# Where the row scales of two head groups are computed: at the recurrence's end, and at attention's own first pass

## The chip, the cores and the metric

One core of one Trainium2 chip runs the whole kernel. The metric is the device time of one execution in microseconds (us); less is better. A profiled execution gives the span from the first to the last instruction and every instruction's start and end. PE is TensorE, ACT is ScalarE, DVE is VectorE, POOL is GpSimd, SP is the queue that issues the DMAs. A number with L is a line of the kernel.

## The reference

One layer of a decoder trunk over 2048 rows of width 1024, in float32. One input projection feeds two head groups: a gated linear recurrence (4 heads of 128) and a stick-breaking attention (8 heads of 64). What the change touches is the normalisation of each group's output by rows, and the output projection behind it:

```python
o_hg = rmsnorm(o_hg, hg_out_norm) * silu(hg)        # 512 columns, eps 1e-6
o_sb = rmsnorm(o_sb, sb_out_norm)                   # 512 columns
mix  = concatenate([o_hg, o_sb], axis=-1) @ w_out   # 1024 x 1024
h    = h + rmsnorm(mix, attn_post_norm)
```

with rmsnorm(x, w) = x * rsqrt(mean(x*x) + eps) * w. The scale rsqrt(mean + eps) is one number a row and group. A dense SwiGLU layer and a gated per-layer embedding follow.

## The kernel before, in words

The 2048 rows are worked in four groups g of 512 rows, and each group in four blocks t of 128 rows. Gains are folded into the operands, and the row scale of a group's half is applied to the product instead of to the operand: half the contraction of the output projection (the recurrence's 512 columns, part 0) is multiplied by the scale of the recurrence's rows, the other half (attention's columns, part 1) by that of attention's rows.

The recurrence (hgrn, L493 to L607) runs head by head. Each head adds the square of its output to a tile acc (L594, L597). After the last head, PE multiplies acc by a column of ones (L605), which gives the sum of squares of each row in the bank hg, and ACT copies these four columns to hgss[:, g, :] (L606), which lives through the whole kernel.

Attention's outputs are loaded by out_load (L612), which writes the operands and adds the squares of attention's half to the tile oss (L626, L629). It is called one group ahead: for g + 1 before the pass of g begins.

The output projection out_proj (L634), called a pass here, starts with sums (L638): four products of oss with the ones in the bank tr (L641), two DVE copies that put the recurrence's sums and attention's sums side by side into the tile rg of eight columns (L643, L644), then on POOL a multiplication and addition (sum / 512 + eps, L645) and a power of -0.5 (L646). Then come four quarters of 256 columns, in each of them part 0 and part 1. A part multiplies four 128x128 blocks by both halves of the rows into two banks of 512 columns. ACT evicts part 0 with the recurrence's scale (L672), DVE adds part 1 with attention's scale (L674). Every product is three matmuls (L224, L225, L226) of operands split into a high part (cast on ACT, L210) and a low part (a subtraction on DVE or POOL, L211).

The order of PE's instructions is written out by hand. The work is cut into steps by generators, and weave (L50) interleaves them: while a pass runs, each of its steps is preceded by a step of attention and one of the recurrence for the next groups, in the passes g = 0 and 1, and by pieces of the normalisation of the mixed rows (post_mix) and of transposes (turn) in later ones. A pass has 32 steps; the first four are part 0 of the first quarter, and the fifth begins part 1. An attention step is either one that makes scores and weights (weights_of, L404: bank z, then ACT L416 and L417, a scan on DVE L431, a product on POOL L435), or one that multiplies the values and turns the next weights (values_of, L459 and L460; turn_of: transposes into the bank tr at L443, read by ACT L446 and DVE L448). A recurrence step makes scores at L525 from a tile qp that POOL updates (L562).

The bank tr has one buffer, for attention's transposes, for the sums and, in the last pass, for every second transpose of turn (L747, read by ACT L752). The bank mm has three.

The other engines' order is not written out: a planner takes instructions, as they become ready in its own model of time, by the order of the program. A tile's new owner waits until the old one's readers are done.

Of the kernel before, what the change touches and what calls it, by code (L numbers as in the profile page):

```python
# [8 lines left out]
F32 = mybir.dt.float32  # L9
# [3 lines left out]
AF = mybir.ActivationFunctionType  # L13
ALU = mybir.AluOpType

P = 128
# [5 lines left out]
TT = GT // P  # L22
HH = 4
# [4 lines left out]
EPS = 1e-6  # L28
# [61 lines left out]
def hybrid_block(  # L90
# [6 lines left out]
    nc = tc.nc  # L97
# [28 lines left out]
    const = ctx.enter_context(tc.tile_pool(name="const", bufs=1))  # L126
# [3 lines left out]
    def ctile(name, shape, dt=F32, pool=const):  # L130
        return pool.tile(list(shape), dt, tag=name, name=name)
# [13 lines left out]
    neghalf = ctile("neghalf", (P, 1))  # L145
# [21 lines left out]
    hgss = ctile("hgss", (P, NG, TT))  # L167
# [6 lines left out]
    def bank(tag):  # L174
        return ps.tile([P, 512], F32, tag=tag, name=tag, bufs=BANKS[tag])
# [12 lines left out]
    def ev(dt=F32, name="ev", shape=(P, GT)):  # L188
        return fb.tile(list(shape), dt, tag="ev", name=name, bufs=12)
# [61 lines left out]
    def dense_op(w_cols, act):  # L251

        ws = [weight(w_cols(kk)) for kk in range(0, HH, 2)]
        banks = []
        for i in range(2):
            banks.append(mm_bank())
            for kk in range(HH):
                mv = [t[:, kk % 2 * 256:(kk % 2 + 1) * 256] for t in ws[kk // 2]]
                for j in range(2):
                    mm3(banks[i][:, j * 256:(j + 1) * 256], cut(act[kk], 2 * i + j), mv,  # L260
                        kk == 0 and j == 0, kk == HH - 1 and j == 1)
                if kk == 1:
                    yield None
            yield banks[i]

    def row_rstd(halves, out=None, ss=None):
        if ss is None:
            ss = const.tile([P, 2], F32, tag="ss", name="ss", bufs=8)
            for j, y in enumerate(halves):
                nc.scalar.activation(junk, y, AF.Square, scale=ROOT, accum_out=ss[:, j:j + 1])  # L270
        r = const.tile([P, 1], F32, tag="ssum", name="ssum", bufs=8)
        nc.gpsimd.tensor_scalar(r, ss[:, 0:1], ss[:, 1:2], EPS, op0=ALU.add, op1=ALU.add)
        if out is None:
            out = const.tile([P, 1], F32, tag="rstd2", name="rstd2", bufs=6)
        nc.gpsimd.tensor_tensor(out, r, neghalf, op=ALU.pow)
        return out
# [216 lines left out]
    def hgrn(g):  # L493
        acc = None
        for h in range(HH):
            def ht(tag, bufs=1, shape=(P, TT, P)):
                return hgp.tile(list(shape), F32, tag=tag, name=tag, bufs=bufs)
# [44 lines left out]
            for w in LEVELS:  # L542
                if w < BL:
                    level(qp, masks[w])
                else:
                    if w == BL:
                        b = bank("hg")
# [30 lines left out]
            for c in range(TT - 1):  # L578
                nc.vector.scalar_tensor_tensor(
                    st[:, c, :], states[-1], last[:, c:c + 1], sbk[:, c * P:(c + 1) * P],  # L580
                    op0=ALU.mult, op1=ALU.add)
# [10 lines left out]
            if h == 0:  # L592
                acc = ht("acc")
# [9 lines left out]
        b = bank("hg")  # L603
        for c in range(TT):
            nc.tensor.matmul(b[:, c:c + 1], acc[:, c, :], ones1, start=True, stop=True)  # L605
        nc.scalar.copy(hgss[:, g, :], b[:, 0:TT])  # L606
        yield  # L607

    HG_STEPS = HH * 11 + 2
# [23 lines left out]

    def out_proj(g, res):  # L634
        ops, acc = res["o"], res["oss"]
        r_hg, r_sb = [], []

        def sums(acc):  # L638
            b = bank("tr")
            for t in range(TT):  # L640
                nc.tensor.matmul(b[:, t:t + 1], acc[:, t * P:(t + 1) * P], ones1, start=True, stop=True)  # L641
            rr = const.tile([P, 2 * TT], F32, tag="rg", name="rg", bufs=2)
            nc.vector.tensor_copy(rr[:, 0:TT], hgss[:, g, :])  # L643
            nc.vector.tensor_copy(rr[:, TT:], b[:, 0:TT])  # L644
            nc.gpsimd.tensor_scalar(rr, rr, 1.0 / (HH * P), EPS, op0=ALU.mult, op1=ALU.add)  # L645
            nc.gpsimd.tensor_tensor(rr, rr, neghalf.to_broadcast((P, 2 * TT)), op=ALU.pow)  # L646
            r_hg.extend(rr[:, t:t + 1] for t in range(TT))
            r_sb.extend(rr[:, TT + t:TT + t + 1] for t in range(TT))

        sums(acc)  # L650
        mix = [[None, None] for _ in range(TT)]
        for quarter in range(4):
            half, o = divmod(quarter, 2)
            if o == 0:
                for t in range(TT):
                    mix[t][half] = ev(name="mix")
            for part in range(2):
                def src(k, part=part, c=quarter * 256):
                    r = (part * HH + k) * P
                    return w_out[r:r + 2 * P, c:c + 256]  # L660

                bank_no = 0
                for b in dense_op(src, ops[part * HH:(part + 1) * HH]):
                    if b is None:
                        yield
                        continue
                    for n in range(2):
                        t = 2 * bank_no + n
                        d = mix[t][half][:, o * 256:(o + 1) * 256]
                        bn = b[:, n * 256:(n + 1) * 256]  # L670
                        if part == 0:
                            nc.scalar.activation(d, bn, AF.Copy, scale=r_hg[t])  # L672
                        else:
                            nc.vector.scalar_tensor_tensor(d, bn, r_sb[t], d, op0=ALU.mult, op1=ALU.add)  # L674
                    bank_no += 1
                    yield
                if g == NG - 1 and o == 1 and part == 1:
                    for t in range(TT):
                        m = mix[t][half]
                        nc.sync.dma_start(h2_s[g][t * P:(t + 1) * P, half * GT:(half + 1) * GT], m)  # L680
                        nc.scalar.activation(junk, m, AF.Square, scale=ROOT, accum_out=sums_m[:, 2 * t + half:2 * t + half + 1])
        res["mix"] = mix
        if g == NG - 1:
            for t in range(TT):
                row_rstd(None, rows_m[t], sums_m[:, 2 * t:2 * t + 2])
# [488 lines left out]
    class Rate:  # L1174
# [29 lines left out]
        ("a", 3, 40, 21), ("b", 2, 52, 26), ("b", 3, 54, 42),  # L1204
    ]
    hgs = [Stream(hgrn(g)) for g in range(NG)]
    spent = 0
    for n, (kind, g, att_n, hg_n) in enumerate(plan):
# [33 lines left out]
    for g in range(NG - 1):  # L1242
        if g + 1 < NG - 1:
            out_load(g + 1, res[g + 1])
        op = Stream(out_proj(g, res[g]))
        if g == 0:
            weave(op, 2, rates.part(2), r2.part(2))
            hgs[2].drain()
            weave(op, OP_SLOTS - 2, rates.part(OP_SLOTS - 2), r3.part(OP_SLOTS - 2))
        elif g == 1:  # L1250
            weave(op, half, rates.part(half), r3.part(half), (pm, TT, 0))
            tu = Stream(turn(un_s[0], u_s[0], g_ffn, ["mm"], xt, ev))
            weave(op, half, rates.part(half), r3.part(half), (tu, 9, 0))
            hgs[3].drain()
            att_stream.drain()
            side.close()
            big[0] = ctx.enter_context(tc.tile_pool(name="bigr", bufs=1, side="right"))
            mm_tags[:] = ["mm", "z", "mm", "z", "mm", "av"]
        else:
            out_load(NG - 1, res[NG - 1])  # L1260
            weave(op, half, (pm, TT, 0))
            weave(op, half, (Stream(first_operands()), ND, 1))
        op.drain()
        pm = Stream(post_mix(g, res[g]["mix"]))

    drive = Drive([(gate_up(0, tt0), 3), (down(0), 4), (gate_up(1, tt1), 3), (down(1), 4),
                   (ple(0, ss0), 5), (ple(1, ss1), 5)])
    drive.prepare(2)
    op = Stream(out_proj(NG - 1, res[NG - 1]))
    tu = Stream(turn(un_s[1], u_s[1], g_ffn, ["tr", "hg"], xt, ev))  # L1270
    weave(op, half + 2, (pm, TT, 0), (tu, 9, 0))
# [40 lines left out]
    for g in range(NG):  # L1312
        stage, step, every, lag, tag = (
            (1, 67, 2, 3, "mm"), (2, 0, 1, 2, "hg"), (3, 67, 2, 3, "mm"), (4, 0, 1, 4, "hg"))[g]
# [35 lines left out]
```

## Time and profile before

| | us |
|---|---|
| median of 3 runs | 3018.2 (3015.58 to 3018.63) |
| the profiled execution's own time | 3020.01 |
| its span, first to last instruction | 3018.0 |
| PE busy | 2913.6 |
| DVE busy | 2086.6 |
| ACT busy | 1579.3 |
| POOL busy | 1431.3 |

The granted clock of TensorE was 0.99 of the full one over the span. In lines of a timeline the first two numbers are the start and the length in us, then engine, line, operation, out<-in by the program's names, the shape, the number of instructions merged; square brackets hold the idle time of that engine just before, and what ended it. In a view of a tile or line, three numbers are the least, median and greatest duration in ns, followed by the first and last start in us. A line of the waits names who waited for whom, the us in total, the times, and the longest. A row of a table by stretches holds the stretch, its length, the busy us of PE, PE's weight loads, DVE, ACT and POOL with their instructions, the granted clock, the DMA share and GB/s.

### The profile page before, as it was taken

How to read it: one execution, taken by the hardware profiler on the slowest of the kernel's cores; microseconds unless marked ns; L12 is line 12 of the kernel's file. 1: busy time of each engine (PE TensorE's matmuls, PEld its weight loads, DVE VectorE, ACT ScalarE, POOL GpSimd, SP SyncE). 2: the span in 40 equal slices, each digit the busy share in tenths (PEclk: the TensorE clock that was granted, in tenths of full speed). 3: DMA queues.
4: the chain of work that ended last, by engine and by line, in shares of the span. 5: the costliest groups of instructions: out<-in, count | busy, mean ns of one | idle time of the engine just before them, and what ended most of it. 6: DMA issues, size and time to landing. Idle time of an engine off the chain costs nothing.

```text
span 3018.0 us, 52849 instructions
## 1 busy us (share of the span) xinstructions
PE 2913.6 (97%) x18280; PEld 2423.3 (80%) x18280; DVE 2086.6 (69%) x2945; ACT 1579.3 (52%) x3188; POOL 1431.3 (47%) x1398
## 2 busy tenths in 40 slices
PE   7999999999999999889998999999999999999998
PEld 6888788878787888789786878888888888878777
DVE  3556666677777776765887787665887775756775
ACT  5666756666667666767523333455433333545532
POOL 3344455545556666865422322445732221456553
PEclk9999999999999999999999999999999999999999
DMA  7775665455445444468767767667955555677974
GB/s 209 223 217 154 177 181 163 148 173 163 142 137 160 146 132 142 160 199 281 260 218 255 248 216 253 208 203 213 344 191 167 173 176 172 213 218 237 321 242 148
DMA packets 469420, 602.28 MB, mean 200 GB/s; under 512 B 43168, under 2 KB 277664, under 8 KB 469152
## 3 DMA queue, kind: packets, MB, share of 16 engines
q1 hardware_dynamic: 469152, 598.91, 63.1%
q8 instruction: 144, 2.36, 0.3%
q14 instruction: 124, 1.02, 0.1%
HBM read 439.89 MB, written 158.86 MB: 198 GB/s over the span
## 4 chain that ended last, share of the span: by engine, by line
PE 45%; DMA 5%; DVE 4%; POOL 2%; issue 2%; ACT 1%; SPq 0%; POOLq 0%; DVEq 0%; ACTq 0%
PE mm L224 6%; PE mm L226 6%; PE mm L225 6%; PE z L226 4%; PE z L225 4%; PE z L224 4%; PE av L226 2%; PE av L225 2%; PE av L224 2%; PE tr L224 2%; PE tr L226 2%; PE tr L225 2%; DVE wl L813 1%; DMA wr<-in_w_out_dram 1%; DVE wr L817 1%
## 5 line engine op out<-in xcount | busy, mean ns | idle before, releaser
L812 ACT CAST wh<-wr 128x512 fp32r<-128x512 f32 x600 | 351.0, 618 | 466.2 <-PE mm L225 185.6
L813 POOL TENSOR_TENSOR wl<-wr,wh 128x512 fp32r<-128x512 f32 x256 | 373.1, 1464 | 444.0 <-ACT wh L812 418.8
L435 POOL TENSOR_TENSOR a<-be,ring 128x512 f32<-128x512 f32 (+2 forms) x320 | 319.1, 998 | 416.0 <-DVE ring L431 394.8
L224 PE MATMUL mm<-uh,wh 128*128 128x512 f32 x1168 | 484.3, 415 | 2.8 <-DVE eb L336 1.8
L226 PE MATMUL mm<-uh,wl 128*128 128x512 f32 x1168 | 460.6, 394 | 0.4 <-POOL wl L211 0.4
L225 PE MATMUL mm<-ul,wh 128*128 128x512 f32 x1168 | 459.0, 393 | 0.0
L813 DVE TENSOR_TENSOR wl<-wr,wh 128x512 fp32r<-128x512 f32 x344 | 302.1, 886 | 172.6 <-ACT wh L812 158.0
L431 DVE TENSOR_TENSOR_SCAN ring<-z,ring,be 128x512 f32<-128x512 f32 x192 | 245.6, 1279 | 107.0 <-ACT z L417 104.1
L224 PE MATMUL mm<-wh,uh 128*128 128x256 f32 (+1 forms) x992 | 307.2, 310 | 9.6 <-ACT uh L812 9.6
L226 PE MATMUL mm<-wh,ul 128*128 128x256 f32 (+1 forms) x992 | 292.1, 294 | 0.0
L225 PE MATMUL mm<-wl,uh 128*128 128x256 f32 (+1 forms) x992 | 292.0, 294 | 0.0
L226 PEld LDWEIGHTS mm<-uh,wl 128*128 128x128 f32 x1168 | 220.4, 189 | 51.6 <-POOL wl L211 0.8
L224 PEld LDWEIGHTS mm<-uh,wh 128*128 128x128 f32 x1168 | 221.8, 190 | 45.4 <-DVE eb L336 2.3
L225 PEld LDWEIGHTS mm<-ul,wh 128*128 128x128 f32 x1168 | 221.8, 190 | 39.8
L210 ACT CAST wh<-wr 128x512 fp32r<-128x512 f32 x288 | 178.3, 619 | 140.0 <-PE mm L225 79.5
L448 DVE TENSOR_TENSOR al<-tr,ah 128x512 fp32r<-128x512 f32 (+1 forms) x320 | 192.3, 601 | 80.7 <-ACT ah L446 79.8
L211 POOL TENSOR_TENSOR wl<-wr,wh 128x512 fp32r<-128x512 f32 x144 | 190.3, 1322 | 108.6 <-ACT wh L210 98.0
L813 POOL TENSOR_TENSOR wl<-s,wh 128x512 fp32r<-128x512 f32 x44 | 95.3, 2171 | 272.2 <-ACT wh L812 249.3
L446 ACT CAST ah<-tr 128x512 fp32r<-128x512 f32 (+1 forms) x320 | 167.7, 524 | 104.3 <-PE tr L443 101.1
L416 ACT ACTIVATE be<-z 128x512 f32<-128x512 f32 (+2 forms) x320 | 171.1, 535 | 84.1 <-PE z L414 35.6
L224 PEld LDWEIGHTS mm<-wh,uh 128*128 128x128 f32 x992 | 190.0, 192 | 18.0 <-ACT uh L812 10.4
L225 PEld LDWEIGHTS mm<-wl,uh 128*128 128x128 f32 x992 | 190.3, 192 | 5.0
(313 smaller groups left out, 7246.5 us busy)
## 6 DMA issues: line engine op xcount, KB each, us to landing
wr<-in_w_gate_up_dram SPq DMA_DIRECT2D x308, 256.0 KB, 3.8
wr<-in_w_in_dram SPq DMA_DIRECT2D x224, 256.0 KB, 3.1
wr<-hid_s SPq DMA_DIRECT2D x154, 256.0 KB, 3.0
wr<-in_w_down_dram SPq DMA_DIRECT2D x110, 256.0 KB, 3.5
hid_s<-hs SPq DMA_DIRECT2D x88, 256.0 KB, 3.5
wr<-wd_s SPq DMA_DIRECT2D x88, 256.0 KB, 3.1
kt<-k_s SPq DMA_DIRECT2D x80, 256.0 KB, 3.1
vt<-v_s SPq DMA_DIRECT2D x80, 256.0 KB, 3.4
```

The costliest lines, as they stand in the source:

```text
L210: nc.scalar.copy(hi, src)
L211: (lo_engine or nc.gpsimd).tensor_tensor(lo, src, hi.bitcast(F32), op=ALU.subtract)
L224: nc.tensor.matmul(o, l[0], r[0], start=start, stop=False)
L225: nc.tensor.matmul(o, l[0], r[1], start=False, stop=False)
L226: nc.tensor.matmul(o, l[1], r[0], start=False, stop=stop)
L416: nc.scalar.activation(be[:, :n], z[:, :n], AF.Sigmoid, scale=0.125)
L431: nc.vector.tensor_tensor_scan(r[:, o:o + n][:, ::-1], z[:, :n][:, ::-1], be[:, :n][:, ::-1], init, op0=ALU.mult, op1=ALU.bypass)
L435: nc.gpsimd.tensor_tensor(a[:, :n], be[:, :n], r[:, o + 1:o + n + 1], op=ALU.mult)
L446: nc.scalar.copy(hi[:, lo_c:], tr[:, lo_c:])
L448: nc.vector.tensor_tensor(lo[:, lo_c:], tr[:, lo_c:], hi[:, lo_c:].bitcast(F32), op=ALU.subtract)
L812: nc.scalar.copy(hi, src)
L813: lo_engine.tensor_tensor(lo, src, hi.bitcast(F32), op=ALU.subtract)
```

## The change

The recurrence's end no longer copies the sums: ACT scales them by 1/512 while it takes them out of the bank, and POOL adds eps and takes the power, in place, so that hgss holds scales. The pass uses them directly. Its sums are made for attention's half alone, when part 1 of the first quarter begins (the fifth step), and the multiplication and addition are done by DVE while it reads the bank; POOL keeps the power, now of four columns.

```diff
@@ hgrn
         for c in range(TT):
             nc.tensor.matmul(b[:, c:c + 1], acc[:, c, :], ones1, start=True, stop=True)
-        nc.scalar.copy(hgss[:, g, :], b[:, 0:TT])
+        r = hgss[:, g, :]
+        nc.scalar.activation(r, b[:, 0:TT], AF.Copy, scale=1.0 / (HH * P))
+        nc.gpsimd.tensor_scalar(r, r, EPS, None, op0=ALU.add)
+        nc.gpsimd.tensor_tensor(r, r, neghalf.to_broadcast((P, TT)), op=ALU.pow)
         yield
@@ out_proj
         ops, acc = res["o"], res["oss"]
-        r_hg, r_sb = [], []
+        r_hg, r_sb = [hgss[:, g, t:t + 1] for t in range(TT)], []
 
         def sums(acc):
             b = bank("tr")
             for t in range(TT):
                 nc.tensor.matmul(b[:, t:t + 1], acc[:, t * P:(t + 1) * P], ones1, start=True, stop=True)
-            rr = const.tile([P, 2 * TT], F32, tag="rg", name="rg", bufs=2)
-            nc.vector.tensor_copy(rr[:, 0:TT], hgss[:, g, :])
-            nc.vector.tensor_copy(rr[:, TT:], b[:, 0:TT])
-            nc.gpsimd.tensor_scalar(rr, rr, 1.0 / (HH * P), EPS, op0=ALU.mult, op1=ALU.add)
-            nc.gpsimd.tensor_tensor(rr, rr, neghalf.to_broadcast((P, 2 * TT)), op=ALU.pow)
-            r_hg.extend(rr[:, t:t + 1] for t in range(TT))
-            r_sb.extend(rr[:, TT + t:TT + t + 1] for t in range(TT))
-
-        sums(acc)
+            rr = const.tile([P, TT], F32, tag="rg", name="rg", bufs=2)
+            nc.vector.tensor_scalar(rr, b[:, 0:TT], 1.0 / (HH * P), EPS, op0=ALU.mult, op1=ALU.add)
+            nc.gpsimd.tensor_tensor(rr, rr, neghalf.to_broadcast((P, TT)), op=ALU.pow)
+            r_sb.extend(rr[:, t:t + 1] for t in range(TT))
+
         mix = [[None, None] for _ in range(TT)]
         for quarter in range(4):
...
             for part in range(2):
+                if quarter == 0 and part == 1:
+                    sums(acc)
+
                 def src(k, part=part, c=quarter * 256):
```

## The prediction

> **What bounds the kernel.** I read the page's totals first.
>
> ```profile
> span 3018.0 us, 52849 instructions
> PE 2913.6 (97%) x18280; PEld 2423.3 (80%) x18280; DVE 2086.6 (69%) x2945; ACT 1579.3 (52%) x3188; POOL 1431.3 (47%) x1398
> ```
>
> TensorE (PE) is the bound: 3018.0 - 2913.6 = 104.4 us without a matmul is all that a better order can win. The change touches the four output projections, g = 0 to 3. Each begins with its sums (L641), the first near 1147 us and the last near 1401; the view of that line and the first pass's piece of the timeline:
>
> ```profile
> L641 PE MATMUL tr<-ones,oss x32: 168/250/352, 1147.0 to 1401.9; 128*128 128x1 f32 x32
> ...
> 1146.95 0.95 PE L641 MATMUL tr<-ones,oss 128*128 128x1 f32 x8
> ```
>
> The table by stretches for 1140 to 1460 us (its sum), and the list of PE's waits there, longest first:
>
> ```profile
> sum 320.00, PE 290.31 PEld 268.92 DVE 212.94 ACT 219.15 POOL 204.09; mean PE 72.58 PEld 67.23 DVE 53.23 ACT 54.79 POOL 51.02
> ...
> PE av L460 <- DVE al L448: 6.1, 2, 4.8
> ...
> PE hg L525 <- POOL qp L562: 2.9, 3, 2.2
> ...
> PE hg L589 <- DVE sl L585: 2.5, 3, 1.1
> ...
> PE tr L747 <- DVE rg L644: 0.8, 1, 0.8
> PE hg L525 <- DVE ks L564: 0.8, 1, 0.8
> ```
>
> PE idles 320 - 290.31 = 29.7 us in these stages, and no row says that PE waits for the sums' input. So the sums' own matmuls (0.95 us a pass, at either place) are neither saved nor added. What can change is who waits for their result, and what they wait for at the new place.
>
> **What the scales cost now.** The view of the tile rg, and the power of a single column from the view of its line:
>
> ```profile
> L643 DVE COPY rg<-hgss x4: 136/166/1027, 597.6 to 1345.2; 128x4 f32<-128x4 f32 x4
> L645 POOL TENSOR_SCALAR rg<-rg x4: 203/390/592, 1150.3 to 1405.9; 128x8 f32<-128x8 f32 x4
> L646 POOL TENSOR_TENSOR rg<-rg,neghalf x4: 1656/1666/1840, 1151.4 to 1406.2; 128x8 f32<-128x8 f32 x4
> ...
> L275 POOL TENSOR_TENSOR rstd<-ssum,neghalf x56: 539/562/1107, 8.9 to 2808.3; 128x1 f32<-128x1 f32 x56
> ```
>
> A power takes 0.562 us for one column and 1.666 for eight, so (1.666 - 0.562)/7 = 0.158 us for each more, and about 0.562 + 3 x 0.158 = 1.04 for four: an estimate from these two medians. POOL now spends 0.39 + 1.67 = 2.06 us a group in one piece at the head of the pass. Afterwards it spends an addition (taken as the same 0.39) and 1.04 at the recurrence's end, and 1.04 later for attention's half: 2.47, or 4 x 0.41 = 1.6 us more in all. It gains only by where it lies. DVE loses four copies, 0.14 to 1.03 us each.
>
> **Pass g = 1, the gain.** POOL, then ACT and PE, and last how PE's bank tr comes free:
>
> ```profile
> 1251.27 0.58 POOL L645 TENSOR_SCALAR rg<-rg 128x8 f32<-128x8 f32 x1
> ...
> 1254.74 1.84 POOL L646 TENSOR_TENSOR rg<-rg,neghalf 128x8 f32<-128x8 f32 x1
> ...
> 1258.85 0.83 POOL L562 TENSOR_TENSOR qp<-qp,pd 128x256 f32<-128x256 f32 x1
> ...
> 1256.61 0.84 ACT L672 ACTIVATE mix<-mm,rg 128x256 f32<-128x256 f32 x2 [2.00 <-POOL rg L646]
> ...
> 1257.02 0.49 PE L443 MATMUL tr<-ident,a 128*128 128x128 f32 x3
> 1259.73 0.46 PE L525 MATMUL hg<-qp,ks 128*32 128x32 f32 x32 [2.22 <-POOL qp L562]
> ...
> 1260.68 0.51 ACT L446 CAST ah<-tr 128x384 fp32r<-128x384 f32 x1
> ...
> 1261.74 0.55 DVE L448 TENSOR_TENSOR al<-tr,ah 128x384 fp32r<-128x384 f32 x1
> ```
>
> ACT's queue stands for 2.00 us at the first eviction (L672) because POOL finishes the power at 1256.58; POOL itself is 0.58 + 1.84 = 2.42 us later at qp, and PE waits 2.22 for qp. With the recurrence's scales ready long before, both waits go: -2.2 us.
>
> But the sums come back at this very place. The second part starts right behind this L525 (fifth step of the pass), and its sums need the only bank tr. The transposes that filled it end at 1257.51, and al has read it at 1261.74 + 0.55 = 1262.29: 4.78 us, of which ACT's 2.00 goes, leaving 2.8. Less the L525 between (0.46), PE waits 2.3. Term: -2.2 + 2.3, taken as 0. Bounds: with the quickest turnaround shown in the next fence it is -2.2 + 0.9 = -1.3; with no relief of ACT -2.2 + 4.3 = +2.1.
>
> **Pass g = 0, the new wait.** Quickest case first, then the place where the fifth step begins:
>
> ```profile
> 1149.74 0.60 PE L443 MATMUL tr<-ident,a 128*128 128x128 f32 x4
> 1151.00 0.69 DVE L448 TENSOR_TENSOR al<-tr,ah 128x512 fp32r<-128x512 f32 x1 [1.02 <-ACT ah L446]
> ...
> 1159.81 0.60 PE L443 MATMUL tr<-ident,a 128*128 128x128 f32 x4
> 1160.34 0.46 PE L525 MATMUL hg<-q,ks 128*32 128x32 f32 x32
> ...
> 1162.05 0.59 ACT L446 CAST ah<-tr 128x512 fp32r<-128x512 f32 x1
> ...
> 1163.23 0.67 DVE L448 TENSOR_TENSOR al<-tr,ah 128x512 fp32r<-128x512 f32 x1
> ```
>
> In the quick case tr is free 1151.69 - 1150.34 = 1.35 us after the transposes; at the new place at 1163.90, or 3.1 us after L525 ends at 1160.80. PE's queue behind the sums holds the second part's matmuls, then the next score matmuls (L410) and recurrence steps: all stand. Nothing is won in this pass, since ACT doesn't wait for rg here. Term: +3.1 (from +0.9, which is 1.35 - 0.46, to +3.1).
>
> **Pass g = 2.** Here POOL lies on the chain:
>
> ```profile
> 1346.26 0.59 POOL L645 TENSOR_SCALAR rg<-rg 128x8 f32<-128x8 f32 x1
> ...
> 1347.83 1.67 POOL L646 TENSOR_TENSOR rg<-rg,neghalf 128x8 f32<-128x8 f32 x1
> ...
> 1350.10 0.30 POOL L272 TENSOR_SCALAR ssum<-ss 128x1 f32<-128x1 f32 x1
> ...
> 1353.59 1.64 POOL L699 TENSOR_TENSOR h<-h,mix 128x512 f32<-128x512 f32 x1 [1.29 <-DVE mix L698]
> 1355.19 1.71 POOL L211 TENSOR_TENSOR wl<-wr,wh 128x512 fp32r<-128x512 f32 x1
> ...
> 1348.58 0.19 ACT L270 ACTIVATION_READ_ACCUMULATOR junk<-mix 128x1 f32 x1
> ...
> 1356.96 0.58 PE L225 MATMUL z<-wl,uh 128*128 128x256 f32 x1 [4.42 <-POOL wl L211]
> ```
>
> PE waits 4.42 us for a weight's low part, which stands on POOL behind additions that wait for the row scale of L272; L645 and L646 (2.26 us) are ahead of it. The square that L272 sums is ready at 1348.77, so L272 can move from 1350.10 by 1.3 us at most: -1.3 (bounds 0 and -2.3). No attention is left in this pass, so tr is free for the sums. The new power (1.04) becomes ready just about when that weight stands on POOL: ahead of it, it takes 1.04, behind it nothing; +0.5. Sum -0.8.
>
> **Pass g = 3.**
>
> ```profile
> 1405.88 0.33 PE L747 MATMUL tr<-ident,xt 128*128 128x128 f32 x1 [0.78 <-DVE rg L644]
> ...
> 1408.91 0.69 ACT L752 ACTIVATE ev<-tr,g_ffn 128x512 f32<-128x512 f32 x1
> ...
> 1409.24 0.60 PE L747 MATMUL hg<-ident,xt 128*128 128x128 f32 x4
> ```
>
> The transposes no longer wait for the sums' copy: -0.8. In turn the sums, behind the second L747, wait until L752 has read tr at 1409.60; since PE arrives there earlier by 0.78 and by the moved sums, between 0 and 1.7 us: +1.0. Sum +0.2.
>
> **The recurrence's ends.** The addition and power (1.43 us, four times) go on POOL where it has pauses; the evictions that read them come later. Cover: POOL's 320 - 204 = 116 idle us here. +0.2 (0 to 1.4, should one stand ahead of a qp).
>
> **The clock.** Granted clock in the stretch behind PE's wait of 2.22 us, and behind that of 4.42:
>
> ```profile
> 1260.00:1263.00 3.00, 3.00 (x39) 2.58 (x25) 2.28 (x5) 3.00 (x9) 2.83 (x3) 0.64 0.27 80
> ...
> 1357.00:1360.00 3.00, 3.00 (x15) 3.00 (x16) 2.43 (x3) 2.47 (x6) 1.59 (x1) 0.53 1.05 397
> ```
>
> So a wait of 2.22 loses another 3.0 x 0.36 = 1.1 us, one of 4.42 loses 1.4. For the new 3.1 at g = 0 I add 1.3 (0 to 1.4); at g = 1 one such wait replaces another. The Trainium skill (TensorE: Matmul & The Clock Gate, Part 1: The HAM clock gate) says that the clock halves after an idle window of about 3.4 us and returns after as long a busy one. By that rule this term is nothing and the sum 1.3 lower; the row behind 2.22 us speaks against the rule's length, so I keep the term.
>
> **What is given back.** While PE stands at g = 0, ACT, DVE and POOL catch up, and the waits listed for sl (2.5) and ks (0.8) shrink: -1.5 of the 3.3 (0 to -3.3).
>
> **Sum:** g = 0: 3.1 + 1.3; g = 1: 0; g = 2: -0.8; g = 3: +0.2; ends +0.2; given back -1.5: +2.5 us. The profiled execution took 3020.01 us (span 3018.0), so 3022.5; the median of the runs is 3018.2, 1.8 less, and on that scale I forecast 3020.7. Against the noise of this kernel (0.2%, or 6 us, is about what a measurement can tell from no change) that is no change. Ends of the terms: low 0.9 - 1.3 - 2.3 - 0.8 - 3.3 = -6.8, high 3.1 + 1.4 + 2.1 + 1.0 + 0.9 + 1.4 = +9.9.
>
> **Rivals.**
> Freed POOL carries (faster). If the planner lets tr be read early, each new wait is 0.9 and costs no clock: g = 0 +0.9; g = 1 -1.3 and its dip's -1.1; g = 2 the full -2.3 and a shorter wait's -1.4; g = 3 -0.8: -6.0, or 3012. For it: POOL is named in the waits of both passes. Against: ACT runs in order and needed 1.6 us to reach ah at g = 0. Chance 0.17.
> The bank tr decides (slower). PE stands behind the sums at full length: +3.1 + 1.4, at g = 1 +2.1 + 0.6, at g = 2 nothing, at g = 3 +0.9, ends +1.4, nothing given back: +9.5, or 3027.7. It decides from a turnaround of about 2.7 us on, since from a wait of 2.2 the clock falls too; both places had more (3.5 and 4.78). Against: the helpers catch up. Chance 0.21.
> The planner re-orders (either sign). Only PE's order is written out; L643 for g = 0 ran at 597.6, far ahead of its pass at 1147. New entries on POOL and ACT shift everything behind, and if a third of the 29.7 idle us moves, that is 10 us either way: 3008 or 3028. Chance 0.08.
>
> **Numbers.** The forecast keeps 0.54. Faster by over 0.2% takes half of the first rival, half of the last and a little of the forecast's edge: 0.14. Slower takes most of the second, half of the last, an edge of the forecast: 0.23. Same: 0.63. The range, 3010 to 3029, holds the sum's two ends (3011.4 and 3028.1) and most of the planner's.
>
> **What would show it.** Right: L641 idle before it on PE at g = 0 and 1, released by DVE al; no ACT wait for a scale at L672; PE's 2.22 for qp gone; 1.0 us for the four-column power. Wrong: no wait at L641, PE's 4.42 at g = 2 gone, or idle time moved in stages that the change doesn't touch, before 1140 or after 1480 us.

## The result, and the profile after

The changed kernel takes 3035.45 us (median of 4 runs, 3033.19 to 3036.23), the kernel before in the same session 3018.41 (4 runs, 3015.58 to 3020.79): a ratio of 1.0051, 95% interval [1.0039, 1.0063]. It is slower by 17 us; I forecast 3020.7 and at most 3029. The profiled execution took 3036.23. The totals of its page:

```profile
span 3034.2 us, 52841 instructions
PE 2920.6 (96%) x18280; PEld 2430.1 (80%) x18280; DVE 2085.6 (69%) x2941; ACT 1578.0 (52%) x3188; POOL 1435.1 (47%) x1402
```

PE is busy 7.0 us longer with the same 18280 matmuls, and the granted clock over the span was 0.987 instead of 0.990; the other 9.2 us of the 16.2 are idle time. The small operations came out as costed, as the views of the tiles rg and hgss show:

```profile
L646 DVE TENSOR_SCALAR rg<-tr x4: 148/162/163, 1170.3 to 1430.4; 128x4 f32<-128x4 f32 x4
L647 POOL TENSOR_TENSOR rg<-rg,neghalf x4: 1011/1016/1041, 1170.6 to 1430.6; 128x4 f32<-128x4 f32 x4
...
L608 POOL TENSOR_SCALAR hgss<-hgss x4: 233/240/244, 597.7 to 1354.9; 128x4 f32<-128x4 f32 x4
L609 POOL TENSOR_TENSOR hgss<-hgss,neghalf x4: 1015/1042/1052, 598.0 to 1355.7; 128x4 f32<-128x4 f32 x4
```

A power of four columns takes 1.02 to 1.04 us. The cost is elsewhere. PE's order is written out, so the n-th matmul of one kernel (sums and fillers left out) is the n-th of the other. I took its start in each profile and subtracted: the difference at a place is the time lost up to there. Worked out so, with places in us of the kernel before, for this kernel and those of the experiments below:

```
                900   1140   1300   1400   1700   3010     span
changed         1.1    2.5   15.4   19.7   16.7   15.7   3034.2
e_again         1.7    2.4   12.0   15.0   12.5   13.4   3031.8
e_head         -0.4    1.6    6.5    6.1    8.6    8.3   3026.8
e_late_only     0.4    2.4    8.3   12.1    9.5    9.9   3028.3
e_step6         1.5    3.8    5.6    8.6    5.2    3.6   3021.9
e_mm_clean      0.8    3.5    5.4    9.6    9.7    9.9   3028.9
e_mm_bank      -0.4    0.9    2.1    5.8    8.0   18.7   3037.4
e_move_only    -0.4    2.2   10.7   15.4   17.0   10.9   3029.7
e_move_mm       1.1    2.0    5.1    9.6   11.7    4.8   3022.8
e_fill          1.2    4.1   10.8   14.8   13.7   21.1   3039.6
e_fill_again    1.2    3.5    9.4   13.4   10.2   17.1   3035.5
e_swap          0.3   -0.1    3.8    4.0   -0.6   -0.4   3017.6
e_actcopy       2.2    1.9    3.1    3.5    3.5    3.1   3021.1
e_ends_only     3.1    4.4    4.4    3.4    4.3    0.3   3019.5
e_read_ends     2.4    2.8    2.7    2.7    2.3   -4.0   3014.0
```

These are single executions; up to 900 us, where hardly anything differs, they lie between -0.4 and 3.1, so a difference under some 3 us says little. The rows changed and e_again are two executions of one kernel, and they differ by 3.3 us between 1140 and 1300 alone. The changed kernel's loss lies where the change is, between 1140 and 1400 us: 17.2 us in the passes g = 0, 1 and 2, and 12.6 in e_again. The table by stretches splits it, first before, then changed over the same matmuls (columns as above):

```profile
1140.00:1240.00 100.00, 92.25 (x1047) 82.05 (x1047) 70.06 (x112) 67.72 (x145) 67.62 (x80) 0.98 0.41 129
1240.00:1300.00 60.00, 52.52 (x575) 46.89 (x576) 45.52 (x69) 45.05 (x104) 49.75 (x61) 0.91 0.56 186
1300.00:1400.00 100.00, 91.35 (x867) 87.18 (x866) 62.47 (x91) 67.17 (x144) 60.74 (x58) 0.97 0.73 239
```

```profile
1142.50:1251.20 108.70, 96.80 (x1047) 85.92 (x1047) 70.94 (x112) 67.70 (x145) 66.80 (x81) 0.93 0.39 119
1251.20:1315.40 64.20, 53.69 (x576) 48.38 (x577) 46.52 (x66) 45.84 (x104) 50.77 (x61) 0.88 0.56 188
1315.40:1419.70 104.30, 93.22 (x866) 88.93 (x865) 61.67 (x91) 66.77 (x143) 59.00 (x57) 0.95 0.67 221
```

The first column after the length is PE's busy time. Pass 0 is 8.7 us longer: 4.15 more idle (11.90 against 7.75) and 4.55 more busy, with the clock at 0.93 instead of 0.98. Pass 1 is 4.2 longer, 3.0 idle and 1.2 busy; pass 2 4.3 longer, 2.4 idle and 1.9 busy. The first two have their main cause in the timeline, at the sums of pass 0 and then of pass 1:

```profile
1165.13 0.46 PE L525 MATMUL hg<-q,ks 128*32 128x32 f32 x32
...
1167.65 0.67 DVE L448 TENSOR_TENSOR al<-tr,ah 128x512 fp32r<-128x512 f32 x1
...
1168.47 1.84 PE L644 MATMUL tr<-ones,oss 128*128 128x1 f32 x8 [2.88 <-DVE al L448]
...
1268.33 0.46 PE L525 MATMUL hg<-qp,ks 128*32 128x32 f32 x32
...
1271.70 0.54 DVE L448 TENSOR_TENSOR al<-tr,ah 128x384 fp32r<-128x384 f32 x1
...
1272.38 1.84 PE L644 MATMUL tr<-ones,oss 128*128 128x1 f32 x8 [3.60 <-DVE al L448]
...
1294.31 1.08 PE L536 MATMUL hg<-qp,ks 128*64 128x64 f32 x8 [2.45 <-DVE ks L564]
```

PE waits 2.88 and 3.60 us for al to read the bank tr, as the rival of the bank had it. The wait for qp in front of L525 is gone (it was 2.22), and a new one of 2.45 for ks has come later in the pass. The longest rows of PE's waits in these two passes, and two shorter ones:

```profile
PE av L460 <- DVE al L448: 6.9, 3, 4.7
PE tr L644 <- DVE al L448: 6.5, 2, 3.6
PE av L459 <- ACT ah L446: 3.3, 2, 2.5
PE hg L536 <- DVE ks L564: 2.4, 1, 2.4
...
PE hg L605 <- POOL acc L597: 0.9, 1, 0.9
...
PE hg L525 <- DVE ks L564: 0.7, 1, 0.7
```

Before, the rows of L460 and L459 were 6.1 and 3.2, and the 0.9 for acc, at the recurrence's end in pass 0, was not there. And the clock ahead of the first of the two waits and behind it, in stretches cut where it changes:

```profile
1160.88:1164.29 3.41, 3.41 (x15) 3.22 (x15) 0.78 (x2) 1.02 (x4) 3.24 (x7) 0.50 0.79 224
...
1167.70:1174.53 6.83, 6.06 (x55) 5.38 (x55) 0.78 (x3) 0.49 (x1) 1.62 (x2) 0.50 0.10 25
```

PE works again from 1168.47, and to 1174.53 the clock is 0.50: about 6.1 us at half speed, so here the wait of 2.88 us costs about another 3.0; the sums themselves take 1.84 us instead of 0.95. In e_again a wait of 3.15 us at the same place cost some 1.7. The low stretch behind it, and then the one behind the 2.22 us of the kernel before:

```profile
1168.00:1171.40 3.40, 3.40 (x17) 3.40 (x17) 0.16 (x1) 0.00 (x0) 1.01 (x1) 0.50 0.12 34
```

```profile
1260.82:1264.23 3.41, 2.93 (x40) 2.21 (x41) 1.47 (x3) 3.06 (x9) 3.23 (x5) 0.50 0.48 140
```

In all sixteen traces a stretch at 0.50 lasts 3.41 us or two to four times that, but for the last one of each trace, which its end cuts short. So the clock behind a wait comes in steps of some 1.7 us of lost work, and a wait of about 3 us cost one step in one execution and nearly two in the other. The stretch from 1160.88 lies ahead of the sums; e_again has none there, so it is no part of the bank's price.

### The profile page after: what moved, and what is told of

Its sections match the earlier page's. It is cut to its first block, busy times and chain, and to the rows that moved or that the text cites. A ratio compares the mean times of both kernels' runs of the same rounds, so it can differ in the third digit from the quotient of the medians.

```text
span 3034.2 us, 52841 instructions
## 1 busy us (share of the span) xinstructions
PE 2920.6 (96%) x18280; PEld 2430.1 (80%) x18280; DVE 2085.6 (69%) x2941; ACT 1578.0 (52%) x3188; POOL 1435.1 (47%) x1402
## 4 chain that ended last, share of the span: by engine, by line
PE 38%; DMA 4%; DVE 3%; issue 2%; POOL 2%; ACT 1%; SPq 0%; POOLq 0%; DVEq 0%; ACTq 0%
PE mm L224 5%; PE mm L226 5%; PE mm L225 5%; PE z L226 3%; PE z L224 3%; PE z L225 3%; PE av L224 2%; PE av L226 2%; PE av L225 2%; PE tr L224 2%; PE tr L226 2%; PE tr L225 2%; DMA wr<-in_w_gate_up_dram 1%; POOL wl L815 1%; DVE wl L815 1%
## 5 line engine op out<-in xcount | busy, mean ns | idle before, releaser
L815 POOL TENSOR_TENSOR wl<-s,wh 128x512 fp32r<-128x512 f32 x44 | 103.1, 2348 | 261.6 <-ACT wh L814 209.2
```

The source lines that it names most:

```text
L815: lo_engine.tensor_tensor(lo, src, hi.bitcast(F32), op=ALU.subtract)
```

## The experiments

Theories: the bank tr with the clock behind its wait (passes 0 and 1); the new work on POOL at the recurrence's ends; the later power in pass 2; and the planner, which orders ACT, DVE and POOL anew whenever an instruction moves. Four sessions; each session's kernels are compared with runs of the kernel before on the same chip.

**First session: one part at a time.** e_head leaves the scales at the recurrence's end and puts attention's sums back at the head of the pass:

```diff
+        sums(acc)
         mix = [[None, None] for _ in range(TT)]
...
-                if quarter == 0 and part == 1:
-                    sums(acc)
```

> The recurrence's scales are made at its end as in the changed kernel, but attention's sums go back to the head of the pass. Theory A (the sums wait in PE's queue for the bank tr, and the clock halves behind that wait): 3013 to 3019 us, no wait at the sums. Theory B (the work added at the recurrence's end on POOL, and what the planner re-orders for it): the loss stays, 3028 to 3036. Theory C (the late power of attention's half stands ahead of weights on POOL in the passes g = 2 and 3): 3028 or more, as passes 0 and 1 would not recover.

e_step6 makes the sums one step later, when attention's next step stands between the transposes and the sums:

```diff
             for part in range(2):
-                if quarter == 0 and part == 1:
-                    sums(acc)
...
                     if b is None:
                         yield
+                        if quarter == 0 and part == 1 and bank_no == 0:
+                            sums(acc)
                         continue
```

> The changed kernel with the sums one step later (sixth step of the pass), still in the bank tr; there the preceding attention step makes scores and no transposes in passes g = 0 and 1. Theory A: no wait of over 1 us at the sums in these passes, 3017 to 3024 us. Theories B and C: as the changed kernel, 3031 to 3038.

e_mm_bank keeps the place and takes a bank of mm through the kernel's own rotation:

```diff
-            b = bank("tr")
+            b = mm_bank()
```

> The changed kernel with the sums written to one of the banks mm instead of tr, at the same place in PE's order. Theory A: no wait at the sums, 3017 to 3024 us, unless the next part then waits for a bank mm. Theories B and C: 3031 to 3038.

e_move_only does the reverse of e_head: the recurrence's end copies as before, the pass computes those scales at its head on POOL (a tile rh of four columns), and only the sums move:

```diff
+        nc.scalar.copy(hgss[:, g, :], b[:, 0:TT])
...
+        rh = const.tile([P, TT], F32, tag="rh", name="rh", bufs=2)
+        nc.gpsimd.tensor_scalar(rh, hgss[:, g, :], 1.0 / (HH * P), EPS, op0=ALU.mult, op1=ALU.add)
+        nc.gpsimd.tensor_tensor(rh, rh, neghalf.to_broadcast((P, TT)), op=ALU.pow)
```

> Only attention's sums move to the fifth step; the recurrence's end copies its sums as before, and their scales are made on POOL at the head of the pass. Theory A: the loss is all there, 3031 to 3039 us. Theory B: it is gone, 3016 to 3022. Theory C: 3025 or more.

Measured against before (3020.95 us): e_head 1.0026 [1.0014, 1.0037], e_step6 1.0020 [1.0010, 1.0029], e_mm_bank 1.0047 [1.0030, 1.0065], e_move_only 1.0025 [1.0013, 1.0036]. Each keeps 0.0020 or more of the 0.0051, so no one part is the whole of it; and by their totals all four miss what I had expected of them if the bank decides. The stages tell more. From 1140 to 1300 the kernels with the wait at tr lose 12.9 (changed) and 8.5 (e_move_only), those without it 1.8 (e_step6) and 1.2 (e_mm_bank). The waits at the sums, first of e_move_only, then of e_step6:

```profile
PE tr L645 <- DVE al L448: 8.7, 2, 5.5
```

```profile
PE tr L644 <- DVE al L448: 0.3, 1, 0.3
```

e_mm_bank can't be read as a whole: it moves the rotation of mm for every later stage, and loses 10.7 us after 1700, where e_mm_clean below, which leaves the rotation, loses 0.2. Its stages up to there can be read.

**Second session: the bank alone, the clock alone, the ends alone, the order alone.** e_mm_clean takes the bank mm without moving the rotation:

```diff
-            b = bank("tr")
+            b = bank("mm" if g < 2 else "tr")
```

> The changed kernel with the sums of passes g = 0 and 1 in a bank mm instead of tr, this time without advancing the rotation of banks that later stages draw from. Theory A (wait for tr and the slow clock behind it are most of the loss, the rest is what the planner re-orders): no wait at the sums, offset of PE's progress against before under 4 us at 1300 us, 3021 to 3028 us. If the wait does not matter to the end: 3032 to 3038.

e_fill leaves the wait and fills it with nine matmuls of 128x512 whose product nobody reads, so that PE isn't idle:

```diff
+FILL = 9
...
                 if quarter == 0 and part == 1:
+                    if g < 2:
+                        fill = bank("mm")
+                        hi = ops[HH][0]
+                        for _ in range(FILL):
+                            nc.tensor.matmul(fill, hi[:, 0:P], hi, start=True, stop=True)
                     sums(acc)
```

> The changed kernel with nine filler products of 128x512 into a bank mm that nobody reads, ahead of the sums in passes g = 0 and 1: PE works for about 2 us of the time in which it would stand for tr. It does more work than the changed kernel. If half of the price of a wait is the clock behind it: the granted clock stays at 1.0 behind the sums, and 3 to 6 us are won against the changed kernel (3028 to 3033). If only the wait counts: the same time or later (3035 to 3038).

e_ends_only is the kernel before with the addition and the power added on POOL at the recurrence's ends, into a tile that nobody reads:

```diff
+    spare = ctile("spare", (P, NG, TT))
...
         nc.scalar.copy(hgss[:, g, :], b[:, 0:TT])
+        r = spare[:, g, :]
+        nc.gpsimd.tensor_scalar(r, hgss[:, g, :], EPS, None, op0=ALU.add)
+        nc.gpsimd.tensor_tensor(r, r, neghalf.to_broadcast((P, TT)), op=ALU.pow)
```

> The kernel before, with the addition and the power of four columns added on POOL at each recurrence's end, into a tile that nobody reads. Theory B (work at the recurrence's end costs): 3025 to 3032, from delays near 596, 932, 1159 and 1339 us. Theory A: only its re-ordering shows, 3017 to 3026, and in places where nothing was added.

e_swap is the kernel before with its two DVE copies in the other order; no instruction differs:

```diff
-            nc.vector.tensor_copy(rr[:, 0:TT], hgss[:, g, :])
             nc.vector.tensor_copy(rr[:, TT:], b[:, 0:TT])
+            nc.vector.tensor_copy(rr[:, 0:TT], hgss[:, g, :])
```

> The kernel before with two independent DVE copies of the sums helper (L643, L644) written in the other order; not one instruction more or fewer, PE's order the same, some 100 to 200 rows of DVE, ACT and POOL in another order. If the planner's order by itself carries several us: off from before by 3 to 9 us, either way. If the order of the helpers is free: within 2 us of before.

Measured (before 3020.19): e_mm_clean 1.0020 [1.0009, 1.0031], e_fill 1.0059 [1.0041, 1.0076], e_ends_only 1.0005 [0.9993, 1.0016], e_swap 1.0013 [1.0002, 1.0024].

With the bank mm the wait is gone and the passes 0 and 1 lose 1.9 us instead of 12.9; the whole kernel is back by 0.0031 of the changed one's 0.0051 (two sessions), about 9 us. One row of its table by stretches, for the matmuls of 1140 to 1300 in the kernel before (160.00 us long there, PE busy 144.78 at a clock of 0.96), and then the view of its sums:

```profile
1143.50:1305.40 161.90, 145.86 (x1622) 129.11 (x1623) 115.51 (x177) 112.98 (x249) 116.85 (x141) 0.96 0.47 150
```

```profile
L644 PE MATMUL mm<-ones,oss x16: 250/250/271, 1166.0 to 1264.8; 128*128 128x1 f32 x16
```

The idle time (16.0 against 15.2) and the clock are those of before: both the wait and its clock hang on the bank.

The fillers keep the clock up in pass 0 and partly in pass 1:

```profile
1166.52 2.33 PE L663 MATMUL mm<-uh 128*128 128x512 f32 x9
1169.74 1.02 PE L645 MATMUL tr<-ones,oss 128*128 128x1 f32 x8 [0.89 <-DVE al L449]
```

The clock behind it, by stretches:

```profile
1168.00:1170.00 2.00, 1.11 (x7) 0.67 (x5) 1.59 (x3) 0.52 (x2) 1.21 (x2) 1.00 0.86 283
1170.00:1172.00 2.00, 2.00 (x18) 2.00 (x19) 0.16 (x1) 0.00 (x0) 0.96 (x1) 1.00 0.40 119
```

The clock is 1.00 where it was 0.50, and although PE does some 4.7 us of unread work more, passes 0 and 1 lose 6.7 us instead of 12.9 (in the repeats below 5.9 instead of 9.6). The price of the clock is real there. Yet the total is no better, since e_fill loses 7.4 us after 1700.

The ends' work costs nothing (-1.0 us from 1140 to 1400). The order alone costs e_swap 3.9 us from 1140 to 1300, given back by 1700; that is little more than the 3.3 between two executions of one kernel, and its total of 1.0013 barely clears no change.

**Third session: repeats and cross terms.** e_again is the changed kernel and e_fill_again is e_fill, both unaltered. e_late_only moves the sums for g = 2 and 3 alone:

```diff
+        if g < 2:
+            sums(acc)
...
-                if quarter == 0 and part == 1:
+                if quarter == 0 and part == 1 and g >= 2:
                     sums(acc)
```

e_move_mm is e_move_only with the sums in the bank mm for g < 2.

> The changed kernel itself, for the same chip and hour as the next three. 3032 to 3038 us if the loss of 0.5% is the kernel's own and not one chip's.

> The kernel with fillers once more, in five rounds beside the changed kernel. If the clock behind the wait is half of the price to the very end: 3 to 6 us under the changed kernel. If what is won in passes 0 and 1 is given back in later stages: within 2 us of it, though PE is 4 us or more ahead at 1300 us.

> The changed kernel with the sums moved only in passes g = 2 and 3 (at the head in g = 0 and 1). Theory A: no wait at tr, so 3022 to 3029 us, like the kernel with all sums at the head. Theory C (the moved power on POOL costs in pass 2): 3 us or more over that kernel, lost between 1340 and 1400 us.

> Sums at the fifth step in a bank mm in passes g = 0 and 1, and the recurrence's scales made at the head of the pass as before: the fourth of the four pairings of place of the scales and bank of the sums. Theory A: no wait, 3017 to 3026 us, some 6 us or more under the same kernel with tr. Theory B: under 3020, since nothing is added at the recurrence's end.

Measured (before 3020.22): e_again 1.0053 [1.0039, 1.0068], e_fill_again 1.0041 [1.0027, 1.0056], e_late_only 1.0035 [1.0022, 1.0048], e_move_mm 1.0009 [1.0000, 1.0018].

The change's loss repeats, with 9.6 us in passes 0 and 1. Moving the bank helps e_move_only too: those passes lose 3.1 instead of 8.5, and the total goes from 1.0025 to 1.0009. The fillers repeat as well: 5.9 us in the two passes and 6.9 lost after 1700. Whether they win as a whole is unclear: e_fill's 1.0059 is above the changed kernel's 1.0051, and e_fill_again's 1.0041 below e_again's 1.0053, with intervals that overlap. After 1700 PE waits for wl, in this list of e_fill's waits from 2100 to 2750 us and then in that of the changed kernel:

```profile
PE z L227 <- DVE wl L821: 3.3, 1, 3.3
PE tr L227 <- DVE wl L821: 3.1, 2, 2.9
```

```profile
PE z L226 <- DVE wl L815: 1.2, 1, 1.2
```

Why fillers at 1167 us should change that at 2150 isn't shown; it stays open.

e_late_only brought the pass that I had missed. Pass 2, from 1300 to 1400, costs +3.0 to +4.7 us in every kernel whose sums stand at the fifth step or, in e_step6, at the sixth (ten of them, the repeats included) and between -1.0 and +0.4 in every one whose sums stand at the head (e_head, e_swap, e_actcopy, e_ends_only, e_read_ends), whatever the bank. e_late_only and e_head differ in nothing but the place of the sums in the passes 2 and 3. No tr wait is there. PE in pass 2 of the kernel before (the wait of 4.42 us at 1356.96 lies between the last two lines), and then PE and POOL in the changed kernel:

```profile
1342.17 0.95 PE L641 MATMUL tr<-ones,oss 128*128 128x1 f32 x8
...
1346.22 0.38 PE L225 MATMUL z<-wl,uh 128*128 128x256 f32 x1 [1.45 <-POOL wl L211]
...
1372.31 0.39 PE L225 MATMUL z<-wl,uh 128*128 128x256 f32 x1 [2.10 <-POOL wl L211]
```

```profile
1361.78 0.38 PE L225 MATMUL z<-wl,uh 128*128 128x256 f32 x1 [2.49 <-POOL wl L211]
...
1367.58 0.95 PE L644 MATMUL tr<-ones,oss 128*128 128x1 f32 x8
...
1369.97 1.02 POOL L647 TENSOR_TENSOR rg<-rg,neghalf 128x4 f32<-128x4 f32 x1
1370.96 1.50 POOL L211 TENSOR_TENSOR wl<-wr,wh 128x512 fp32r<-128x512 f32 x1
...
1372.51 0.58 PE L225 MATMUL z<-wl,uh 128*128 128x256 f32 x1 [2.33 <-POOL wl L211]
...
1381.13 0.39 PE L225 MATMUL av<-wl,uh 128*128 128x256 f32 x1 [0.97 <-POOL wl L211]
...
1387.45 0.39 PE L225 MATMUL z<-wl,uh 128*128 128x256 f32 x1 [1.74 <-DVE wl L211]
...
1392.05 0.39 PE L225 MATMUL z<-wl,uh 128*128 128x256 f32 x1 [2.91 <-POOL wl L211]
```

At the head of the pass PE waits for a weight's low part from POOL, 1.45 us behind the sums and 2.49 without them: the sums filled a wait there. At the fifth step they take 0.95 us again, and the power of 1.02 us stands directly ahead of the next weight on POOL. Yet PE pays for neither up to there: it goes on from both waits 15.6 us behind the kernel before (1346.22 and 1361.78, 1356.96 and 1372.51), and ahead of them it was 15.4 behind. The loss comes at the weights after that, for which PE waits three times (0.97, 1.74 and 2.91 us) where it had waited once (2.10). Worked out as the table above:

```
                1340   1358   1373   1400
changed         15.4   15.5   19.7   19.7
e_again         12.0   11.9   15.4   15.0
e_late_only      8.3    8.1   12.5   12.1
e_head           6.5    6.2    6.0    6.1
e_swap           3.8    3.7    4.0    4.0
```

From 1358 to 1373 all ten kernels lose 3.5 to 5.6 us, and the other five between -1.6 and +1.1. The idle time adds up: +1.04 us at the first wait, -2.09 at the second, +3.52 behind them, against 2.4 measured over the pass. The 1.9 us of busy time are about what one more low stretch costs: there are three of 3.41 us in the pass (from 1362.27, 1372.51 and 1392.98), and two before. By which path the later sums make those weights late isn't shown. ACT, DVE and POOL, which prepare them, run in another order there, and no run took the power alone from its place.

**Fourth session: what e_head's loss is.** e_head has no moved matmul and less work on POOL at the head, yet stands at 1.0026. e_read_ends is the kernel before with the scales computed at the ends too, and the evictions of part 0 reading those; the pass still computes all eight columns:

```diff
+    spare = ctile("spare", (P, NG, TT))
...
+        r = spare[:, g, :]
+        nc.gpsimd.tensor_scalar(r, hgss[:, g, :], 1.0 / (HH * P), EPS, op0=ALU.mult, op1=ALU.add)
+        nc.gpsimd.tensor_tensor(r, r, neghalf.to_broadcast((P, TT)), op=ALU.pow)
...
-            r_hg.extend(rr[:, t:t + 1] for t in range(TT))
+            r_hg.extend(spare[:, g, t:t + 1] for t in range(TT))
```

> The kernel before with addition and power added at each recurrence's end, as in the kernel with the ends' work alone, but the evictions of part 0 now read these scales instead of rg; the pass keeps all its work, eight columns, at its head. The only thing taken away is the evictions' wait for the pass's power. If the early scales help by themselves: 2 us or more under the kernel with the ends' work alone. If what the planner makes of it decides: anywhere from 3016 to 3030 us, with PE's offset arising in stretches of the other helpers (930 to 960, 1240 to 1300 us).

e_actcopy is the kernel before with one copy of four columns on ACT instead of DVE:

```diff
-            nc.vector.tensor_copy(rr[:, 0:TT], hgss[:, g, :])
+            nc.scalar.copy(rr[:, 0:TT], hgss[:, g, :])
```

> The kernel before with one copy of four columns (L643) on ACT instead of DVE, 0.15 us of work moved four times. If the planner's order by itself carries several us: off from before by 2 to 8 us either way, arising where the order differs. If not: within 2 us.

Measured (before 3020.71): e_read_ends 0.9986 [0.9974, 0.9998], e_actcopy 1.0002 [0.9993, 1.0010]. Reading the scales early takes nothing: e_read_ends stands in all three passes where before stands (2.8 to 2.7). Nor does it win there; its 6.3 us come after 1700, in stages that it doesn't touch. So what is left of e_head's loss is neither the ends' work nor the early scales; by elimination it is the order that the planner makes once L645 is gone from POOL and L643 from DVE. e_head loses 4.9 us from 1140 to 1300, and e_late_only, which has its sums at the head there too, 5.9. In e_head's waits of these passes al stands longer than in before's (6.1, 2, 4.8):

```profile
PE av L460 <- DVE al L448: 8.9, 4, 4.9
```

An order alone moved these passes by 3.9 us in e_swap and by 1.2 in e_actcopy, each in a single execution, where two executions of one kernel differ by 3.3. That it costs e_head and e_late_only their 4.9 and 5.9 is argued, not shown.

## Why the prediction was wrong

**The wait at g = 0** was right: 3.1 forecast, 2.88 measured and 3.15 in e_again, released by DVE al. **The clock behind it** was mis-sized: 1.3 us, where it cost about 3.0, and 1.7 in e_again. The price had been read from a stretch of 3 us that ended at 1263, while the clock stayed low up to 1264.23; and that a low stretch can last twice as long was not in the term. Pass 0 as a whole lost 4.15 idle and 4.55 at the clock, against a forecast of 3.1 and 1.3; of this the wait for acc (0.9) and the low stretch ahead of the sums (about 1.7) are no part of the bank.

The Trainium skill's rule (TensorE: Matmul & The Clock Gate, Part 1: The HAM clock gate), an idle window of about 3.4 us ahead of a halved clock, doesn't hold by this trace if it is read, as I did, as an idle time of that length: idle times of 2.88, 2.49 and 2.33 us were each followed by a lowered clock (0.50 behind the first). Its other half, a busy stretch of about the same 3.4 us until full speed is back, agrees with the low stretches of 3.41 us in pass 2, while pass 0 took two of them.

**Pass g = 1** failed in "-2.2 + 2.3, taken as 0". The relief came as forecast: no wait of ACT for a scale at the first eviction (L672, now L674) is listed any more, and PE's 2.22 for qp is gone. But the new wait was 3.60 us instead of 2.3, the clock over the pass was lower (0.88 against 0.91 before), and a wait of 2.45 for ks came behind them. I had subtracted ACT's 2.00 us from the turnaround of tr, as though an engine that is freed would be freed for this. ACT had in fact written ah at 1269.81, but DVE took other work ahead of al:

```profile
1269.35 0.46 ACT L446 CAST ah<-tr 128x384 fp32r<-128x384 f32 x1
...
1270.49 1.28 DVE L564 TENSOR_TENSOR ks<-ks,tree 128x256 f32<-128x256 f32 x1
```

So al had read the bank only at 1271.70 + 0.54 = 1272.24, 3.45 us after L525 ended.

**Pass g = 2** had the wrong sign: -0.8 forecast, +4.3 measured (+3.0 in the repeat). The step that failed is that the sum for this pass ends at the weight of the 4.42 us, with -1.3 won there. That wait did shrink, to 2.33, but the one ahead of it grew from 1.45 to 2.49 and the sums came back between them, so that PE stood as before (+0.1 from 1340 to 1358) and nothing was gained. The weights behind it, which were put at nothing without a reason, cost 4.2 us (3.5 in the repeat). That the sums' own 0.95 us are "neither saved nor added" came out up to that weight. The power, priced at +0.5, did stand ahead of the weight as its upper bound had it, and moved PE by nothing that shows there.

**What is given back** (-1.5) wasn't. Of the waits that were to shrink, the one for ks at L525 is there at its old length (0.7 us, 0.8 before), and that for sl too, in PE's waits of these stages of the changed kernel (2.5 before):

```profile
PE hg L589 <- DVE sl L585: 2.4, 4, 1.1
```

What came back, 3.0 us, came between 1400 and 1700 (19.7 to 16.7), in stages that I hadn't named.

**The recurrence's ends** were right: +0.2 forecast, nothing measured. **g = 3** can't be told: 0.2 forecast, -0.8 from 1400 to 1460.

**The rivals.** "The bank tr decides" had the mechanism: with the wait for tr (and no fillers in it) the passes 0 and 1 lose 8.5 to 12.9 us, without it 1.2 to 3.1. It was priced at 3027.7, too low by the rest of the clock and by pass 2, both of which it lacked. "Freed POOL carries" falls by e_head, where POOL sheds that work at the head of the pass and no pass gains. The planner's rival stands beside the others and not in their place: the 4.9 and 5.9 us of e_head and e_late_only in passes 0 and 1 have no other cause that the runs left standing, which is less than shown.

No version beats both kernels clearly. e_read_ends is below before by 0.0014, but it gains that in stages that have nothing to do with the change.

## What to carry to other kernels

Ask of an instruction that is moved in an ordered queue what its output buffer waits for at the new place, and what hid it at the old one: the same 0.95 us of sums met no wait at the head of a pass and one of about 3 us a few steps later, in a bank with one buffer, and another bank took that wait away. Price a new wait on TensorE by the clock too: here one of about 3 us cost another 1.7 or 3.0. Follow a moved instruction past the next wait: in pass 2 all was even there, and the loss came at the weights behind it. Two executions of one kernel differed by 3.3 us in a stage, so compare stages one by one, and over many kernels, ahead of the totals.

## What the runs showed of the hardware

The four kernels that hold one more small tile (128x16 or twice 128x4 elements) are faster by 4 to 7 us behind 1700 us, as the table shows for e_ends_only, e_read_ends, e_move_only and e_move_mm between 1700 and 3010; of the others none but e_step6 (1.6) is by more than 1.0. The same group of matmuls from 1970 to 2110 us, before and then in e_ends_only (after the bar the busy us and the mean ns of one):

```profile
L225 PE MATMUL mm<-wl,wh 128*128 128x512 f32 x78 | 30.9, 396 | 0.0
```

```profile
L226 PE MATMUL mm<-wl,wh 128*128 128x512 f32 x85 | 33.0, 388 | 0.0
```

And these 140 us in the table by stretches, again before and then e_ends_only:

```profile
1970.00:2110.00 140.00, 140.00 (x602) 112.63 (x601) 85.67 (x109) 73.04 (x134) 72.46 (x55) 1.00 0.70 208
```

```profile
1970.00:2110.00 140.00, 140.00 (x613) 114.89 (x612) 81.73 (x105) 71.72 (x129) 72.59 (x53) 1.00 0.69 213
```

With no idle time and the clock at 1.00, PE gets through 613 matmuls instead of 602, and the one product shown takes 388 ns instead of 396 (the other two of each three change by 2 ns at most). What the extra tile changes isn't shown; the other tiles may lie elsewhere in memory then, and the traces hold no addresses. It means that the totals of e_move_only, e_move_mm, e_ends_only and e_read_ends are flattered by about that much, and that the stages are the better measure here. The price of a power on POOL, 0.562, 1.016 and 1.666 us for one, four and eight columns, is a straight line within 0.02 us.
